# Self-attention of a decoder layer: heads in pairs, scores in two row halves, value product turned round, group norm on transposed outputs

## The chip, the cores and the metric

The kernel runs on one core of a Trainium2 chip. The metric is device time in microseconds (us) of one launch; lower is better. Engines: PE is TensorE (matmuls; its weight loads are shown apart as PEld), DVE is VectorE, ACT is ScalarE, POOL is GpSimd, SP is SyncE, which issues nearly all DMAs here.

## The reference, cut to what matters

One decoder layer on 256 tokens of 1024 features: a SwiGLU half step, self-attention with 16 heads of 64, cross-attention to 256 memory tokens, a second SwiGLU half step, a final norm. The change touches the self-attention alone. For each head h with its queries, keys and values (256 x 64 each) the kernel computes

```
s   = q k^T / 8 + bias(distance) + log(multiplicity)     # -1e30 where the key is later than the query
p   = exp(s - max(s));   o = (p @ v) / sum(p)            # 256 queries x 64
ya  = o of heads 0..11,  times 1/rms over its 768 features, times g_out_a
yb  = o of heads 12..15, times 1/rms over its 256 features, times g_out_b
x   = x + concat(ya, yb) @ w_out
```

The three dilated patterns of heads 0 to 11 fold into one softmax by the log of the number of patterns that reach a key; heads 12 to 15 see one own block of 256 keys. So all 16 heads are the same work with different bias tables.

## The kernel before, in words

Residual x lives transposed (features on partitions, 256 tokens along the row) in eight tiles `X`. Every large product is taken in two float32r parts (a rounded part and the remainder, `split` and `wsplit`), as `mm2` (L201 to L203: one matmul of 512 columns and one of 256) or `mm3` (L185 to L187). Weights come in loads of 0.5 MB; ACT (L122) and DVE (L123) split each into its two parts, up to eight chunks ahead.

The queries and keys of a group of eight heads lie transposed in a slot: head pair j in columns 256 j to 256 j + 255, its even head on partitions 0 to 63 and its odd one on 64 to 127. The values lie with tokens on partitions. These small products are plain float32.

`attend` is side work. The main stream (`qkv(1)` while group 0 attends; `cross_k` and `cross_v(0)` while group 1 does) calls `tick` after each product, which moves a clock in us and fires whatever `later` has put in its list by then. So a head's steps stand between main-stream matmuls in PE's queue. A scheduler then orders the instructions of every engine by its own estimate of when each is ready, and each engine works through its list in that order. For each head:

- `scores` (L448, L449): two matmuls with 64 rows of the array, 128 and 256 columns; DVE adds the bias and takes the maximum (L455, L457); ACT takes exp and the sum (L459).
- `turn` (L466, L469): three 128x128 transposes of p on PE, copied out of PSUM by DVE.
- `pv` (L475 to L477): three matmuls with p^T as the stationary operand (128 columns) and 64 columns of values moving; results gather in two PSUM banks held for the whole group.

After head 7 `finish` divides by the sums. After group 1 `out_norm` takes both groups' sums of squares on ACT, (mean + eps)^-0.5 on POOL, and scales O on DVE; `transposed` then turns O in 16 transposes (L516) and splits it times the gain. `addT(w_out, ..)` follows once all four slots of the result are asked for. `Stats` is the helper for norms on transposed data: `add` squares on ACT and adds on POOL, `_col` sums over partitions by a matmul with ones (L329), takes the power on POOL (L334) and builds two diagonal tiles on DVE (L338); `_rows` spreads them over partitions by a second matmul (L344) that DVE copies out (L346).

Of the kernel before, what the change touches and what calls it, by code (L numbers as in the profile page):

```python
# [13 lines left out]
OP = mybir.AluOpType  # L14
# [14 lines left out]
def layer_kernel(ctx, tc, x_in, mem_in, g_ffn1, w_gu1, w_dn1, g_mix, w_in, rel_bias, g_out_a, g_out_b,  # L29
# [98 lines left out]
    def colchunk(wd, c0, n, nkt=KT):  # L128
        """split tiles of n columns: per k-tile (tile, offset)."""
# [9 lines left out]
    def colchunk2(wd, c0, c1):  # L139
        """256 columns at c0 beside 256 columns at c1."""  # L140
# [49 lines left out]
    def act(slots, k):  # L190
        """hi and lo [128, 256 tokens] of k-tile k."""
# [14 lines left out]
    def mmT(ps, wk, xs, k, blk, start, stop):  # L206
        """ps[128 columns of block blk, 256 tokens] += w^T x for k-tile k, as two halves if ps is [128, 512]."""
# [8 lines left out]
    def mmT_wide(pieces, wk, xs, k, start, stop):  # L216
        """mmT of all blocks, each in its own bank, part by part."""
# [8 lines left out]
    def projT(wk, xs, nblk, spread=False, whole=0, abreast=False):  # L226
        """the transposed product block by block; in halves but for the last blocks."""
# [22 lines left out]
    def halves(out, ps):  # L250
        """out = the sum of the halves of ps."""
# [4 lines left out]
    def scaled(out, pieces, R, scale=None):  # L256
        """out = pieces side by side, times the rows R."""
# [23 lines left out]
    def proj(ps, wk, xs, tb, n=512):  # L281
        """ps[128 tokens of block tb, n columns]."""
# [7 lines left out]
    def split(s, k, nk, src, g=None):  # L290
        """k-tiles k, k + 1, .. of the slot from src [128, nk x 256]."""
# [10 lines left out]
    class Stats:  # L302
        """sum of squares over features, then 1/rms as a column per token block and as rows."""

        def __init__(self):
# [20 lines left out]
        def _col(self):  # L326
# [5 lines left out]
            nc.vector.tensor_scalar(ms, ps[:, 0:4:2], 1.0 / D, 1e-6, OP.mult, OP.add)  # L332
# [26 lines left out]
    def next_x(gname):  # L359
        """splitter of finished residual blocks for the next normalised product."""  # L360
# [53 lines left out]
    def addT(wd, src, block):  # L414
        """X += wd^T src over 8 k-tiles."""
# [22 lines left out]

    def attend(g, q, k, v, O, lsum, every, then=None, wait=1.0):
        """side work: one head after another, `every` us apart."""  # L440
        po = [bank(), bank()]

        def scores(hl):
            h = g * 8 + hl
            rows = slice((hl % 2) * 64, (hl % 2) * 64 + 64)
            o = (hl // 2) * 256
# [4 lines left out]
            pt = work.tile([P, 384], F32, tag="pt", name="pt", bufs=4)  # L451
            mx = small.tile([P, 2], F32, tag="mx", name="mx")
            nm = small.tile([P, 2], F32, tag="nm", name="nm")
            for tb, c, n, fo in ((0, 0, 128, 128), (1, 128, 256, 0)):
                nc.vector.tensor_tensor_reduce(pt[:, c:c + n], sp[:, c:c + n], F[h // 8][:, h % 8, fo:fo + n],  # L455
                                               1.0, -3.0e38, OP.add, OP.max, mx[:, tb:tb + 1])
            nc.vector.tensor_scalar(nm, mx, -1.0, None, OP.mult)  # L457
            for tb, c, n in ((0, 0, 128), (1, 128, 256)):
                nc.scalar.activation(pt[:, c:c + n], pt[:, c:c + n], AF.Exp, bias=nm[:, tb:tb + 1],  # L459
                                     accum_out=lsum[tb][:, h:h + 1])  # L460
            later(4.0, turn, hl, pt)

        def turn(hl, pt):
            tp = bank()
            for i in range(3):
                nc.tensor.transpose(tp[:, i * P:(i + 1) * P], pt[:, i * P:(i + 1) * P], ident)  # L466
            tick(0.33)
            pT = work.tile([P, 384], F32, tag="pT", name="pT", bufs=2)
            nc.vector.tensor_copy(pT, tp[:, :384])  # L469
            later(2.0, pv, hl, pT)  # L470

        def pv(hl, pT):
            oc = slice(hl * 64, hl * 64 + 64)
            oc1 = slice(512 + hl * 64, 512 + hl * 64 + 64)
            nc.tensor.matmul(po[0][:, oc], pT[:, 0:128], v[:, oc], start=True, stop=True)  # L475
# [381 lines left out]
```

## Time and profile before

| what | us |
| --- | --- |
| time, median of 3 runs (lowest to highest) | 627.78 (627.72 to 627.87) |
| profiled execution, its span | 626.8 |
| the median over the span | 0.98 |
| PE busy, share of the span | 616.6, 98% |
| weight loads busy, share | 545.6, 87% |
| DVE, ACT, POOL busy | 443.4, 344.2, 39.1 |
| PE's share of the chain that ended last | 95% |

Busy time of PE is the time in which some matmul was under way; matmuls overlap their fill and drain, so the duration of one is longer than what it adds to the stream. What one adds is read from the starts of its neighbours. The self-attention stands between 235.7 and 336 us of the span.

### The profile page before, as it was taken

How to read it: one execution, taken by the hardware profiler on the slowest of the kernel's cores; microseconds unless marked ns; L12 is line 12 of the kernel's file. 1: busy time of each engine (PE TensorE's matmuls, PEld its weight loads, DVE VectorE, ACT ScalarE, POOL GpSimd, SP SyncE). 2: the span in 40 equal slices, each digit the busy share in tenths (PEclk: the TensorE clock that was granted, in tenths of full speed). 3: DMA queues.
4: the chain of work that ended last, by engine and by line, in shares of the span. 5: the costliest groups of instructions: out<-in, count | busy, mean ns of one | idle time of the engine just before them, and what ended most of it. 6: DMA issues, size and time to landing. Idle time of an engine off the chain costs nothing.

```text
span 626.8 us, 10024 instructions
## 1 busy us (share of the span) xinstructions
PE 616.6 (98%) x3806; PEld 545.6 (87%) x3806; DVE 443.4 (71%) x743; ACT 344.2 (55%) x597; POOL 39.1 (6%) x52
## 2 busy tenths in 40 slices
PE   8999999999999999999999999999999999999996
PEld 7987888888999988887788998889888888889985
DVE  4888648887576665866768797878688787784415
ACT  6766436564555257545566766757464564654313
POOL 0000200000011102100001220003000000000000
PEclk9999999999999999999999999999999999999998
DMA  6867995677565554254335463634555656475401
GB/s 228 282 209 240 218 241 185 210 246 238 185 197 171 166 189 149 79 181 145 101 94 186 158 218 98 192 104 137 196 176 195 201 178 213 147 266 185 155 0 68
DMA packets 58992, 110.07 MB, mean 176 GB/s; under 512 B 3760, under 2 KB 14864, under 8 KB 58944
## 3 DMA queue, kind: packets, MB, share of 16 engines
q1 hardware_dynamic: 57952, 106.02, 52.5%
q0 software_dynamic: 832, 2.88, 2.7%
q8 instruction: 30, 0.49, 0.3%
q10 hardware_dynamic: 160, 0.53, 0.2%
q14 instruction: 18, 0.15, 0.1%
HBM read 107.58 MB, written 1.84 MB: 175 GB/s over the span
## 4 chain that ended last, share of the span: by engine, by line
PE 95%; DVE 1%; issue 1%; DMA 1%; ACT 0%; POOL 0%; POOLq 0%; SPq 0%; DVEq 0%
PE bank L202 38%; PE bank L203 19%; PE bank L185 8%; PE bank L186 8%; PE bank L187 8%; PE bank L222 7%; PE bank L449 1%; PE bank L448 1%; PE bank L466 1%; DMA raw<-in_w_ffn_gu_dram 1%; DVE w L123 1%; PE bank L516 1%; PE bank L477 1%; PE bank L476 1%; PE bank L475 0%
## 5 line engine op out<-in xcount | busy, mean ns | idle before, releaser
L202 PE MATMUL bank<-slot,w 128*128 128x512 f32 x1000 | 358.5, 402 | 0.0
L123 DVE TENSOR_TENSOR w<-raw,w 128x1024 fp32r<-128x1024 f32 (+1 forms) x197 | 237.5, 1218 | 75.6 <-ACT w L122 73.9
L203 PE MATMUL bank<-slot,w 128*128 128x256 f32 x1000 | 281.0, 281 | 0.0
L122 ACT ACTIVATE w<-raw 128x1024 fp32r<-128x1024 f32 (+1 forms) x197 | 202.3, 1050 | 105.0 <-PE bank L187 41.7
L202 PEld LDWEIGHTS bank<-slot,w 128*128 128x128 f32 x1000 | 187.9, 188 | 49.3 <-issue 4.6
L203 PEld LDWEIGHTS bank<-slot,w 128*128 128x128 f32 x1000 | 189.0, 189 | 0.1
L185 PE MATMUL bank<-w,slot 128*128 128x512 f32 (+1 forms) x196 | 67.7, 346 | 0.0
L186 PE MATMUL bank<-w,slot 128*128 128x512 f32 (+1 forms) x196 | 67.2, 343 | 0.0
L187 PE MATMUL bank<-w,slot 128*128 128x512 f32 (+1 forms) x196 | 66.9, 341 | 0.0
L253 ACT ACTIVATE hv<-bank 128x256 f32<-128x256 f32 x108 | 40.2, 375 | 43.0 <-PE bank L203 41.5
L222 PE MATMUL bank<-slot,w 128*128 128x256 f32 x432 | 55.4, 285 | 1.3 <-ACT w L122 1.3
L222 PEld LDWEIGHTS bank<-slot,w 128*128 128x128 f32 x432 | 52.8, 191 | 1.8 <-ACT w L122 1.5
L187 PEld LDWEIGHTS bank<-w,slot 128*128 128x128 f32 x196 | 36.9, 188 | 4.5
L185 PEld LDWEIGHTS bank<-w,slot 128*128 128x128 f32 x196 | 37.0, 189 | 4.4
L186 PEld LDWEIGHTS bank<-w,slot 128*128 128x128 f32 x196 | 37.1, 189 | 3.8
L185 PE MATMUL bank<-slot,w 128*128 128x256 f32 x120 | 34.0, 284 | 0.0
L187 PE MATMUL bank<-slot,w 128*128 128x256 f32 x120 | 34.0, 283 | 0.0
L186 PE MATMUL bank<-slot,w 128*128 128x256 f32 x120 | 34.0, 283 | 0.0
L296 ACT ACTIVATE slot<-u 128x512 fp32r<-128x512 f32 x22 | 13.9, 630 | 34.3 <-DVE u L390 34.2
L254 DVE TENSOR_TENSOR u<-bank,hv 128x256 f32<-128x256 f32 x40 | 16.8, 420 | 13.6 <-ACT hv L253 13.5
L300 DVE SCALAR_TENSOR_TENSOR slot<-X,gT,slot 128x256 fp32r<-128x256 f32 x30 | 21.1, 722 | 5.1 <-ACT slot L299 5.0
L185 PEld LDWEIGHTS bank<-slot,w 128*128 128x128 f32 x120 | 23.0, 192 | 0.1
(140 smaller groups left out, 549.4 us busy)
## 6 DMA issues: line engine op xcount, KB each, us to landing
raw<-in_w_ffn_gu_dram SPq DMA_DIRECT2D x88, 512.0 KB, 4.8
raw<-in_w_ffn_down_dram SPq DMA_DIRECT2D x44, 512.0 KB, 4.4
raw<-in_w_ckv_dram SPq DMA_DIRECT2D x16, 512.0 KB, 4.7
raw<-in_w_in_dram SPq DMA_DIRECT2D x12, 512.0 KB, 3.7
raw<-in_w_in_dram SPq DMA_DIRECT2D x24, 256.0 KB, 4.2
raw<-in_w_out_dram SPq DMA_DIRECT2D x8, 512.0 KB, 4.3
raw<-in_w_cq_dram SPq DMA_DIRECT2D x8, 512.0 KB, 5.5
raw<-in_w_co_dram SPq DMA_DIRECT2D x8, 512.0 KB, 5.2
```

The lines of the kernel that those rows point to most:

```text
L122: nc.scalar.activation(w[:, 0, a:b], raw[:, a:b], AF.Copy)
L123: nc.vector.tensor_tensor(w[:, 1, a:b], raw[:, a:b], w[:, 0, a:b].bitcast(F32), OP.subtract)
L185: nc.tensor.matmul(ps, ah, bh, start=start, stop=False)
L186: nc.tensor.matmul(ps, al, bh, start=False, stop=False)
L187: nc.tensor.matmul(ps, ah, bl, start=False, stop=stop)
L202: nc.tensor.matmul(ps, wh, xhl, start=start, stop=False)
L203: nc.tensor.matmul(ps[:, :256], wl, xhl[:, :256], start=False, stop=stop)
L222: nc.tensor.matmul(ps, w[:, wp_, o + blk * P:o + (blk + 1) * P], a, start=start and i == 0, stop=stop and i == 2)
L253: nc.scalar.activation(t, ps[:, 256:], AF.Copy)
L254: nc.vector.tensor_tensor(out, ps[:, :256], t, OP.add)
L296: nc.scalar.activation(h, src, AF.Copy)
L300: nc.vector.scalar_tensor_tensor(l, src, g, h.bitcast(F32), OP.mult, OP.subtract)
```

## The change

Heads go in pairs. `scores(j)` issues the four matmuls of heads 2j and 2j+1 alternately: 128 columns of the even head (rows 0 to 63 of the array, its own PSUM bank), 128 of the odd (rows 64 to 127, another bank), then 256 and 256. Probabilities are divided by their sum before the transposes, on POOL (32 `tensor_scalar`). `pv(j)` holds 64 columns of values stationary and streams p^T (256 and 128 columns), the even head into partitions 0 to 63 of one bank and the odd into 64 to 127, so that the output is already transposed. No PSUM bank is held over a group. `pv(j)` of pairs 0 and 1 stands right behind the scores of pair j+2; of pairs 2 and 3 some 2.5 us behind their transposes. Of the two copies of p^T one is now ACT's. The norm of the two groups uses `Stats` on the transposed outputs, the first (768 features) after pair 5, the second after pair 7; `out_split` applies 1/rms and gain and splits. `finish`, `out_norm` and the 16 transposes of O go. (The full diff also drops comments and docstrings.)

```
-        def scores(hl):
-            sp = bank()
-            nc.tensor.matmul(sp[:, 0:128], q[rows, o:o + 128], k[rows, o:o + 128], start=True, stop=True)
-            nc.tensor.matmul(sp[:, 128:384], q[rows, o + 128:o + 256], k[rows, o:o + 256], start=True, stop=True)
...
-            later(4.0, turn, hl, pt)
...
-            nc.tensor.matmul(po[0][:, oc], pT[:, 0:128], v[:, oc], start=True, stop=True)
-            nc.tensor.matmul(po[1][:, oc], pT[:, 128:256], v[:, oc], start=True, stop=False)
-            nc.tensor.matmul(po[1][:, oc], pT[:, 256:384], v[:, oc1], start=False, stop=True)
+        def scores(j):
+            rows = (slice(0, 64), slice(64, 128))
+            sp = [bank(), bank()]
+            for c, n, t in ((0, 128, 0), (128, 256, 128)):
+                for e in range(2):
+                    nc.tensor.matmul(sp[e][:, c:c + n], q[rows[e], o + t:o + t + 128], k[rows[e], o:o + n],
+                                     start=True, stop=True)
+            tick(0.6)
+            if j > 1:
+                pv(j - 2)
...
+                nc.vector.reciprocal(rl, l)
+                for tb, c, n in ((0, 0, 128), (1, 128, 256)):
+                    nc.gpsimd.tensor_scalar(pt[:, c:c + n], pt[:, c:c + n], rl[:, tb:tb + 1], 1.0, OP.mult, OP.mult)
+                pts[j].append(pt)
+            later(8.0, turn, j)
...
+        def pv(j):
+            op = bank()[:, :256]
+            for kb, c, n in ((0, 0, 256), (1, 256, 128)):
+                for e in range(2):
+                    vc = kb * 512 + (j * 2 + e) * 64
+                    nc.tensor.matmul(op[e * 64:e * 64 + 64, 256 - n:256], v[:, vc:vc + 64], pTs[j][e][:, c:c + n],
+                                     start=kb == 0, stop=kb == 1)
+            nc.vector.tensor_copy(OT[g][:, j * 256:j * 256 + 256], op)
+            done(g * 4 + j, op)
...
+    def head_pair(kt, op):
+        st = stA if kt < 6 else stB
+        st.add(op)
+        if kt == 5:
+            st.done(delay=3.0)
+            later(8.0, lambda: out_split(OT, stA.rows(), range(3), ot))
+        elif kt == 7:
+            st.done(delay=3.0)
+            later(8.0, lambda: out_split(OT, stB.rows(), range(3, 4), ot))
```

On PE, one head of group 1 as it stood before: scores (L448, L449), a main-stream product (L202, L203: `mm2`), the value product of the head before (L475 to L477).

```order
L448 MATMUL bank<-slot 128x128
L449 MATMUL bank<-slot 128x256
L202 MATMUL bank<-slot,w 128x512
L203 MATMUL bank<-slot,w 128x256
L475 MATMUL bank<-slot,pT 128x64
L476 MATMUL bank<-slot,pT 128x64
L477 MATMUL bank<-slot,pT 128x64
```

On PE now, pair 2 of group 1 at the same place: L451 are the scores of both heads, L498 the value product of pair 0, L202 and L203 the main stream.

```order
L451 MATMUL bank<-slot 128x128 x2
L451 MATMUL bank<-slot 128x256 x2
L498 MATMUL bank<-pT,slot 64x256 x2
L498 MATMUL bank<-pT,slot 64x128 x2
L202 MATMUL bank<-slot,w 128x512
L203 MATMUL bank<-slot,w 128x256
```

Two heads' scores now stand next to each other, alternating between the halves, and the value product of another pair right behind them, with no main-stream product between.

On PE, the end of the attention before: the last products of `cross_v(0)` (L185 to L187: `mm3`) and the 16 transposes of O (L516).

```order
L185 MATMUL bank<-w,slot 128x512
L186 MATMUL bank<-w,slot 128x512
L187 MATMUL bank<-w,slot 128x512
L516 MATMUL bank<-ident,slot 128x128 x16
L185 MATMUL bank<-w,slot 128x512
L186 MATMUL bank<-w,slot 128x512
L187 MATMUL bank<-w,slot 128x512
```

On PE now, the same place: L330 and L345 are the two steps of the second group's `Stats` (L329 and L344 before), and the first L202 is the first product of `addT(w_out, ..)`.

```order
L185 MATMUL bank<-w,slot 128x512
L330 MATMUL bank<-ones,ssq 128x2 x2
L186 MATMUL bank<-w,slot 128x512
L187 MATMUL bank<-w,slot 128x512
L185 MATMUL bank<-w,slot 128x512
L186 MATMUL bank<-w,slot 128x512
L187 MATMUL bank<-w,slot 128x512
L345 MATMUL bank<-dg,ones 128x128 x2
L202 MATMUL bank<-slot,w 128x512
L203 MATMUL bank<-slot,w 128x256
```

The transposes are gone; five matmuls of `cross_v(0)` stand between the two steps of the norm, and behind the second nothing is left of `cross_v(0)`.

On DVE now, what lies around those two steps: L333 turns the sums into mean squares, L339 builds the diagonals, L347 copies the rows R, L513 and L297 are `out_split` of the last two tiles; L123 are weight splits and L584 a split of the cross values.

```order
L333 TENSOR_SCALAR ms<-bank 128x2
L123 TENSOR_TENSOR w<-raw,w 128x1024
L339 TENSOR_SCALAR dg<-ident,col 128x128 x2
L584 SCALAR_TENSOR_TENSOR slot<-bank,col,slot 128x512
L347 COPY R<-bank 128x256
L123 TENSOR_TENSOR w<-raw,w 128x1024
L513 SCALAR_TENSOR_TENSOR og<-slot,gT,R 128x256 x2
L123 TENSOR_TENSOR w<-raw,w 128x1024
L297 TENSOR_TENSOR slot<-og,slot 128x2x256
```

On DVE before, the corresponding place: mean squares (L504) and the scaling of O (L507) of the second block of tokens, then weight splits and the splits of the transposed O (L300).

```order
L504 TENSOR_SCALAR oms<-oss 128x1
L573 SCALAR_TENSOR_TENSOR slot<-bank,col,slot 128x512
L507 TENSOR_SCALAR slot<-slot,or 128x768
L507 TENSOR_SCALAR slot<-slot,or 128x256
L123 TENSOR_TENSOR w<-raw,w 128x1024 x2
L300 SCALAR_TENSOR_TENSOR slot<-bank,gT,slot 128x256 x5
```

A chain through DVE, POOL, DVE, PE, DVE and ACT now ends in `addT`, with three weight splits between its steps.

## Rows read from the trace of the kernel before

**Rows 1.** The page, parts 1 and 2: busy time of each engine; PE's share, granted clock in slices.
```profile
PE 616.6 (98%) x3806; PEld 545.6 (87%) x3806; DVE 443.4 (71%) x743; ACT 344.2 (55%) x597; POOL 39.1 (6%) x52
PE   8999999999999999999999999999999999999996
...
PEclk9999999999999999999999999999999999999998
```

**Rows 2.** The page, part 4: the chain that ended last, by engine.
```profile
PE 95%; DVE 1%; issue 1%; DMA 1%; ACT 0%; POOL 0%; POOLq 0%; SPq 0%; DVEq 0%
```

**Rows 3.** Timeline of PE, one head: start us, us, engine, line, operation, tiles, shape, count.
```profile
303.34 0.28 PE L203 MATMUL bank<-slot,w 128*128 128x256 f32 x1
...
303.70 0.28 PE L203 MATMUL bank<-slot,w 128*128 128x256 f32 x1
303.90 0.49 PE L448 MATMUL bank<-slot 64*128 64x128 f32 x2
304.23 0.59 PE L449 MATMUL bank<-slot 64*128 64x256 f32 x2
304.75 0.50 PE L202 MATMUL bank<-slot,w 128*128 128x512 f32 x1
305.09 0.28 PE L203 MATMUL bank<-slot,w 128*128 128x256 f32 x1
...
306.11 0.28 PE L203 MATMUL bank<-slot,w 128*128 128x256 f32 x1
306.23 0.49 PE L466 MATMUL bank<-ident,pt 128*128 128x128 f32 x3
...
306.79 0.28 PE L203 MATMUL bank<-slot,w 128*128 128x256 f32 x1
```

**Rows 4.** Timeline of the weight loads (PEld) in the same stretch.
```profile
303.90 0.29 PEld L448 LDWEIGHTS bank<-slot 64*128 64x128 f32 x2 [0.25 <-issue]
304.12 0.30 PEld L449 LDWEIGHTS bank<-slot 64*128 64x128 f32 x2
304.75 0.19 PEld L202 LDWEIGHTS bank<-slot,w 128*128 128x128 f32 x1 [0.33 <-issue]
```

**Rows 5.** Timeline of PE, the transposes of O and their neighbours.
```profile
333.94 0.40 PE L187 MATMUL bank<-w,slot 128*128 128x512 f32 x1
334.17 1.91 PE L516 MATMUL bank<-ident,slot 128*128 128x128 f32 x16
...
336.15 0.40 PE L186 MATMUL bank<-w,slot 128*128 128x512 f32 x1
```

**Rows 6.** Timeline of PE, two norms by `Stats` (L329, L344) in the main stream.
```profile
204.86 0.50 PE L329 MATMUL bank<-ones,ssq 128*128 128x2 f32 x4
205.22 3.36 PE L222 MATMUL bank<-slot,w 128*128 128x256 f32 x26
208.42 0.60 PE L344 MATMUL bank<-dg,ones 128*128 128x128 f32 x4
208.78 0.49 PE L222 MATMUL bank<-slot,w 128*128 128x256 f32 x2
...
435.84 0.51 PE L329 MATMUL bank<-ones,ssq 128*128 128x2 f32 x4
...
440.08 0.68 PE L344 MATMUL bank<-dg,ones 128*128 128x128 f32 x4 [0.64 <-DVE dg L338]
```

**Rows 7.** Timeline of DVE between the steps of the first of these norms.
```profile
206.96 0.48 DVE L338 TENSOR_SCALAR dg<-ident,col 128x128 f32<-128x128 f32 x2 [0.83 <-POOL col L334]
```

**Rows 8.** Timeline of ACT, the end of the same head's exp.
```profile
307.08 0.50 ACT L459 ACTIVATE pt<-pt,nm 128x256 f32<-128x256 f32 x1
```

**Rows 9.** Timeline: POOL's addition of squares, and a weight split on DVE beside it.
```profile
251.51 0.73 POOL L317 TENSOR_TENSOR ssq<-ssq,sq 128x256 f32<-128x256 f32 x1 [0.44 <-ACT sq L312]
...
251.65 1.68 DVE L123 TENSOR_TENSOR w<-raw,w 128x1024 fp32r<-128x1024 f32 x1
```

**Rows 10.** Groups by line and shape on DVE, two of them: count, busy us, mean ns.
```profile
L123 DVE TENSOR_TENSOR w<-raw,w 128x1024 fp32r<-128x1024 f32 x195 | 236.1, 1223 | 74.0 <-ACT w L122 72.4 <-DMA rbt<-in_rel_bias_dram 0.5
...
L297 DVE TENSOR_TENSOR slot<-kn,slot 128x512 fp32r<-128x512 f32 x4 | 2.7, 685 | 0.0
```

More of the change, by code (lines that the diff above doesn't have):

```diff
@@ L331, in _col @@
             ms = small.tile([P, 2], F32, tag="ms", name="ms")
-            nc.vector.tensor_scalar(ms, ps[:, 0:4:2], 1.0 / D, 1e-6, OP.mult, OP.add)
+            nc.vector.tensor_scalar(ms, ps[:, 0:4:2], 1.0 / self.n, 1e-6, OP.mult, OP.add)
             self.col = small.tile([P, 2], F32, tag="col", name="col")
@@ L437, in qkv @@
         return q, k, v
-    def attend(g, q, k, v, O, lsum, every, then=None, wait=1.0):
-        po = [bank(), bank()]
-        def scores(hl):
-            h = g * 8 + hl
-            rows = slice((hl % 2) * 64, (hl % 2) * 64 + 64)
-            o = (hl // 2) * 256
-            sp = bank()
-            nc.tensor.matmul(sp[:, 0:128], q[rows, o:o + 128], k[rows, o:o + 128], start=True, stop=True)
-            nc.tensor.matmul(sp[:, 128:384], q[rows, o + 128:o + 256], k[rows, o:o + 256], start=True, stop=True)
-            tick(0.65)
[L451 to L460, printed above, removed]
-            later(4.0, turn, hl, pt)
[L463 to L474, printed above, removed]
-            nc.tensor.matmul(po[0][:, oc], pT[:, 0:128], v[:, oc], start=True, stop=True)
-            nc.tensor.matmul(po[1][:, oc], pT[:, 128:256], v[:, oc], start=True, stop=False)
-            nc.tensor.matmul(po[1][:, oc], pT[:, 256:384], v[:, oc1], start=False, stop=True)
-            tick(0.33)
-            if hl == 7:
-                finish()
-        def finish():
-            for tb in range(2):
-                rl = small.tile([P, 8], F32, tag="rl", name="rl")
-                nc.vector.reciprocal(rl, lsum[tb][:, g * 8:g * 8 + 8])
-                nc.vector.tensor_tensor(O[tb][:, g * 512:g * 512 + 512].rearrange("p (h e) -> p h e", e=64),
-                                        po[tb].rearrange("p (h e) -> p h e", e=64),
-                                        rl.unsqueeze(2).broadcast_to([P, 8, 64]), OP.mult)
-            if then is not None:
-                then()
-        for hl in range(8):
-            later(wait + hl * every, scores, hl)
@@ new lines, in out_split @@
+    def out_split(OT, R, js, ot):
+        for j in js:
+            t = work.tile([P, 512], F32, tag="g1", name="og", bufs=3)
+            for i in range(2):
+                kt = j * 2 + i
+                nc.vector.scalar_tensor_tensor(t[:, i * 256:i * 256 + 256],
+                                               OT[kt // 4][:, (kt % 4) * 256:(kt % 4) * 256 + 256], gain("out", kt),
+                                               R, OP.mult, OP.mult)
+            s = slot()
+            split(s, 0, 2, t)
+            ot.append(s)
@@ L728, in layer_kernel @@
     st.done()
-    O = [slot(F32), slot(F32)]
-    lsum = [work.tile([P, 16], F32, tag=f"l{tb}", name=f"l{tb}", bufs=1) for tb in range(2)]
+    OT = [slot(F32), slot(F32)]
+    stA, stB = Stats(768), Stats(256)
+    ot = []
+    def head_pair(kt, op):
[7 more added lines that the diff above has]
+            later(8.0, lambda: out_split(OT, stB.rows(), range(3, 4), ot))
     qkv0 = qkv(0, xs, st)
-    attend(0, *qkv0, O, lsum, 4.0)
+    attend(0, *qkv0, OT, 7.0, head_pair)
     mxs, mst = mem_side()
     qkv1 = qkv(1, xs, st)
-    ot = []
-    def normed():
-        out_norm(O)
-        later(7.5, transposed, lambda kt, tb: O[tb][:, kt * P:(kt + 1) * P], "out", None, None, ot)
-    attend(1, *qkv1, O, lsum, 3.3, normed)
+    attend(1, *qkv1, OT, 6.0, head_pair)
     K = cross_k(mxs, mst)
```

50 lines of the change are left out of this document (37 added, 13 removed).

## The prediction

> **What bounds the kernel now.** I read the page's busy times first, then the chain that ended last, then PE's timeline. PE is busy 616.6 of 626.8 us with the granted clock at full level in nearly every slice [rows 1], the level of 2.4 GHz, and 95% of the chain that ended last is PE [rows 2]. So the time is the length of PE's list plus what PE waits. DVE has 71%, ACT 55%, POOL 6% [rows 1]: work moved to them costs only if PE comes to wait for it.
>
> What an item adds to PE's list is read from the starts of the main stream's matmuls around it, not from durations. Undisturbed, one L203 follows the last after 0.36 us (303.34 to 303.70) [rows 3]. With a head's scores between them it is 1.39, so scores cost 1.03; with a head's value product 1.02, so 0.66; with three transposes 0.68, so 0.32 [rows 3]. Sixteen heads: 16 x (1.03 + 0.66) = 27.0 us for scores and value products. The transposes of p stay 48 in number and are left out.
>
> **What the 1.03 consists of.** Each plain float32 matmul shows as two records (x2): two passes, each with its own weight load [rows 3, 4]. The two loads of L448 take 0.29 together where one takes 0.19, so loads start 0.1 to 0.11 apart, and a pass of 128 columns also adds 0.11: L448 to L449 is 0.33, one load and two passes. A pass of 256 columns I take as twice that, 0.22; two of them fill 0.44 of the 0.52 from L449 to L202 [rows 3]. The passes of one head make 0.66; the other 0.37 of the 1.03 go in changing to 64 rows and back. The loads sit idle 0.25 before and 0.33 behind the scores for "issue", that is for nothing that waits on another engine [rows 4]; between 128-row matmuls this isn't seen. I call it a change of shape, 0.19 each way.
>
> The Trainium skill (TensorEngine Tiling (Array Packing), Key Properties) says that changing the tiling mode drains the engine. The idle 0.25 and 0.33 agree. By that rule the new value product, with 64 columns stationary, pays as well, though the old one did not; without the rule the sum below would come out up to 3 us lower.
>
> **Scores and value products after.** Two heads have 1.32 of passes for the scores (four of 0.11, four of 0.22), and the value product has the same: two heads of 256 and 128 columns, two passes each. With nothing beside anything a session is 1.32 + 0.37 = 1.69. If the halves were wholly parallel it would be 0.66 + 0.37 = 1.03. Between them: the two passes of one matmul use the same half and follow each other, so only the second pass of one head can lie beside the first pass of the other. In the issued order the value product then takes 0.22 x 3, then 0.11 x 2 = 0.88, with the change 1.25. For the scores the same pairing gives 0.88, but each pass needs a load of 128 columns, and no two loads in rows 4 start closer than 0.1; in line at 0.11 they hold the passes back to 1.09, with the change 1.46. The trace shows neither half next to the other nor a stationary of 64 columns, so both ends stay in the range: 1.03 to 1.69 for each session. For the change of the value product the ends are 0 (the old one) and 0.37; I take 0.37, the row of the other narrow shape. I take the middle case, since the loads' spacing is the nearest row. In four of the eight pairs the value product stands right behind scores, which saves one change out of four each: 4 x 0.19 = 0.7.
>
> Sum: 8 x (1.46 + 1.25) - 0.7 = 21.0, against 27.0: -6.0 us.
>
> **Norm.** The 16 transposes of O cost 2.21 - 2 x 0.23 = 1.75 (L187 at 333.94 to L186 at 336.15, two matmuls apart) [rows 5]. Each new `Stats` adds two items of 0.36 (204.86 to 205.22, 208.42 to 208.78) [rows 6], two of them 1.4. Net -0.3.
>
> **New waits of PE.** None of the old steps made PE wait noticeably. Now:
> - Second group's norm. Between L330 and L345 stand five matmuls, so L345 is due 0.36 + 5 x 0.23 = 1.5 behind L330. In the trace the diagonals were done 2.6 behind L329 at best (207.44 to 204.86) [rows 6, 7], and at worst L344 came 4.24 behind, after a wait of 0.64 shown on the weight loads [rows 6]. A weight split (1.22) [rows 10] stands between the same steps on DVE's list now. PE waits 1.1 to 2.7; I take 2.0, and everything behind it in PE's list, `addT`, waits along.
> - The last tile of `out_split`. It is asked for 12 products, 4.3 us, behind L345. The chain is L345 0.4, the copy of R 0.4, a weight split 1.2, two scalings 0.8, a second weight split 1.2 beside ACT's rounding, and the subtraction 0.7 [rows 10] (the pieces of 256 columns are taken as 0.4, from the 0.69 of 512): 4.7. 0 to 1.2; I take 0.5.
> - First group's norm. Its last addition on POOL stands behind the scaling of pair 7's probabilities. 0 to 1.0; 0.5.
> - Transposes of a pair. One head's exp ended 3.7 us behind the start of its scores (307.58 to 303.90) [rows 3, 8]. For the second head of a pair add its longer scores 0.7, its place behind the first on DVE 0.9, a weight split in front of its reciprocal 1.2, and on POOL 0.4 + 0.7 for each head (the 0.73 of an addition over 256 columns as upper bound [rows 9], less below): 8.7. In the order some 19 main products and two sessions lie between, 9.5 us. So it is hidden with 0.8 to spare, less than one weight split of 1.22. Over eight pairs 0 to 6; I take 1.0.
>
> Together +4.0. ACT and DVE gain some 2 us of work each over the 100 us of the attention, POOL about 24; DVE at 71% and POOL nearly idle there cover this, and without that cover it would come as the last wait in the list.
>
> Sum: -6.0 - 0.3 + 4.0 = -2.3. The profiled execution has a span of 626.8 and the median is 627.8, 1.0 around it; the same around the new span gives 627.8 - 2.3 = **625.5**.
>
> **Rivals.**
> 1. The halves are wholly parallel, or nearly. Scores and value products take 8 x 2.06 - 0.7 = 15.8: -11.2, with the rest 620.3. For it: two heads touch disjoint rows and banks. Against: in rows 3 and 4 a half-height matmul still shows both passes and both loads in line. The Trainium skill (TensorE: Matmul & The Clock Gate, Part 3: Packing small matmuls) states for tiles in different row groups that they start about 4 ns apart and take little more than one of them; by it alone the two heads' scores would cost one head's. No run here shows that yet. Chance 0.17.
> 2. Slower: nothing overlaps. Sessions of 1.69 make 8 x 3.38 - 0.7 = 26.3, -0.7 in all, and the waits of +4.0 decide: 627.8 - 0.7 - 0.3 + 4.0 = 630.8. It decides as soon as the overlap gives under 3.3 of its 6 us. For it: a load and a pass of the same head stand between any two instructions of different heads but one, and in rows 3 and 4 everything of L448 and L449 goes in line. Chance 0.17.
> 3. Only the row halves overlap, the value product doesn't, since both its heads need all 128 rows: 8 x (1.46 + 1.69) - 0.7 = 24.5, -2.5; 629.0. Chance 0.12.
> 4. The softmax comes late. A weight split took 1.68 instead of 1.22 beside an addition of POOL [rows 9, 10]: the two engines hold each other up. With 32 scalings more on POOL and the margin of 0.8 above, each pair would be 1 us late: 8 instead of 1: 632.5. The Trainium skill (SBUF — State Buffer, Who interferes with whom) says that a DVE instruction with two inputs in SBUF and a GpSimd one that reads SBUF exclude each other; the 1.68 agrees. Chance 0.10.
>
> **How the numbers follow.** The forecast has 0.44, over 623 to 628 with its waits of 1 to 6. What a measurement of this kernel can tell from no change is 0.2%, 1.3 us, so faster means below 626.5 and slower above 629.0. Faster: 0.33 of the forecast, 0.17 of rival 1, 0.01 of rival 3: 0.51. Within 0.2%: 0.09 of the forecast, 0.02 of rival 2, 0.06 of rival 3, 0.01 of rival 4: 0.18. Slower: 0.02 of the forecast, 0.15 of rival 2, 0.05 of rival 3, 0.09 of rival 4: 0.31. The range reaches from rival 1 to rival 2: 620.5 to 630.8.
>
> **What will show it.** L451: sessions of about 1.5 us for two heads, from L203 to L203 less 0.36, with the odd head's first pass starting at the even head's second. L498: 1.25, with idle loads for "issue" around it. L345: a wait of about 2 us for the diagonals on DVE. L482: waits for POOL in few pairs. The prediction is wrong if sessions stand near 1.03 or 1.69, if PE waits more than 6 us between 235 and 340, or if that stretch of PE's list changes elsewhere.

## The result, and the profile after

| what | us |
| --- | --- |
| time after, median of 4 runs (lowest to highest) | 623.1 (621.92 to 624.2) |
| before, beside it | 627.82 (627.72 to 627.87) |
| ratio | 0.9923, 95% interval 0.9912 to 0.9935 |
| profiled execution of after, its span | 623.77, 622.0 |

Faster by 4.7 us, where 2.3 were forecast. Page of after, parts 1 and 2, against [rows 1]:

```profile
PE 608.2 (98%) x3774; PEld 536.5 (86%) x3774; DVE 443.2 (71%) x755; ACT 345.7 (56%) x601; POOL 61.7 (10%) x90
...
PE   8999999999999999899998999999999999999995
...
PEclk9999999999999999999997999999999999999999
```

PE is busy 8.4 us less, but the span is only 4.8 shorter: there are two slices with an 8 in PE's row where there was none, and the clock row has a 7. Part 4, against [rows 2], shows PE's share of the chain fallen from 95% to 91%:

```profile
PE 91%; DVE 2%; ACT 2%; issue 2%; POOL 1%; DMA 1%; POOLq 0%; SPq 0%; DVEq 0%; ACTq 0%
```

**Scores and value products.** Timeline of PE, the value product of a pair alone, the scores of a pair alone, and further on the scores of a pair with the value product of another behind them (compare [rows 3]):

```profile
276.17 0.39 PE L187 MATMUL bank<-w,slot 128*128 128x512 f32 x1
276.49 0.87 PE L498 MATMUL bank<-pT,slot 128*64 128x256 f32 x8
277.29 0.50 PE L185 MATMUL bank<-w,slot 128*128 128x512 f32 x1
277.63 0.40 PE L186 MATMUL bank<-w,slot 128*128 128x512 f32 x1
...
284.19 0.28 PE L203 MATMUL bank<-slot,w 128*128 128x256 f32 x1
284.40 0.93 PE L451 MATMUL bank<-slot 64*128 64x128 f32 x8
285.26 0.50 PE L202 MATMUL bank<-slot,w 128*128 128x512 f32 x1
285.59 0.28 PE L203 MATMUL bank<-slot,w 128*128 128x256 f32 x1
...
297.55 0.28 PE L203 MATMUL bank<-slot,w 128*128 128x256 f32 x1
297.76 0.93 PE L451 MATMUL bank<-slot 64*128 64x128 f32 x8
298.61 0.87 PE L498 MATMUL bank<-pT,slot 128*64 128x256 f32 x8
299.41 0.50 PE L202 MATMUL bank<-slot,w 128*128 128x512 f32 x1
299.75 0.28 PE L203 MATMUL bank<-slot,w 128*128 128x256 f32 x1
```

From L203 to L203 the scores of two heads take 1.40, less 0.36: 1.04 (1.05 in the mean of four). One head took 1.03 before. The eight records of two heads are busy for 0.93; the four of one head, L448 and L449 of [rows 3], reach from 303.90 to 304.82, 0.92. So the second head costs next to nothing (0.01 to 0.02). In the single records behind the row both heads' first passes start 0.007 apart, then both second passes, and so on; the loads likewise. The value product of a pair alone adds 0.99 to 1.00 (here 1.46 from L187 to L186, less two steps of 0.23); scores and value product together add 1.85 (2.20 less the 0.35 of an undisturbed step), 0.19 less than apart.

Timeline of the weight loads in the second of these stretches, against [rows 4]:

```profile
297.75 0.52 PEld L451 LDWEIGHTS bank<-slot 64*128 64x128 f32 x8 [0.26 <-issue]
298.61 0.63 PEld L498 LDWEIGHTS bank<-pT,slot 128*64 128x64 f32 x8 [0.33 <-DVE w L123]
```

The idle time at each change of shape is still there, 0.26 and 0.33 as before. (That 0.33 is named after a DVE split, but the same 0.33 stands as "issue" behind scores without a value product.)

Over the eight pairs scores and value products take 15.6 us, where the sixteen heads took 27.2: -11.6.

**Where part of it went.** PE at the norm of the second group, after (L330 and L345 are L329 and L344 of [rows 6]):

```profile
326.42 0.39 PE L185 MATMUL bank<-w,slot 128*128 128x512 f32 x1
327.45 0.61 PE L330 MATMUL bank<-ones,ssq 128*128 128x2 f32 x4 [0.64 <-POOL ssq L318]
...
328.92 0.40 PE L187 MATMUL bank<-w,slot 128*128 128x512 f32 x1
331.27 1.23 PE L345 MATMUL bank<-dg,ones 128*128 128x128 f32 x4 [1.95 <-DVE dg L339]
...
333.57 0.63 PE L202 MATMUL bank<-slot,w 128*128 128x512 f32 x1
334.00 0.41 PE L203 MATMUL bank<-slot,w 128*128 128x256 f32 x1
334.21 0.63 PE L202 MATMUL bank<-slot,w 128*128 128x512 f32 x1
```

POOL and DVE between the two steps:

```profile
329.28 1.61 POOL L335 TENSOR_TENSOR col<-ms,mhalf 128x2 f32<-128x2 f32 x1 [1.89 <-DVE ms L333]
```
```profile
329.06 0.14 DVE L333 TENSOR_SCALAR ms<-bank 128x2 f32<-128x2 f32 x1
329.13 1.21 DVE L123 TENSOR_TENSOR w<-raw,w 128x1024 fp32r<-128x1024 f32 x1
330.93 0.48 DVE L339 TENSOR_SCALAR dg<-ident,col 128x128 f32<-128x128 f32 x2 [0.59 <-POOL col L335]
```

L330 to L345 is 3.8 us: DVE reaches the mean 1.6 after L330, POOL's power takes 1.6 beside a weight split, and the diagonals follow. Five products (1.2 us) cover it. L330 costs 0.9 more than the 0.44 that such a step adds without a wait (0.36 for itself, 0.08 on the product behind it), the wait at L345 2.2. And then the products are slow: L202 to L202 is 0.64 (333.57 to 334.21) instead of 0.35. Stretches of 2 us there, with the granted clock in the third column from the right:

```profile
330.00:332.00 2.00, 0.73 (x3) 0.73 (x4) 1.41 (x4) 0.04 (x1) 0.90 (x1) 0.57 0.75 250
332.00:334.00 2.00, 2.00 (x8) 1.71 (x7) 1.54 (x3) 1.06 (x1) 0.00 (x0) 0.50 0.73 215
...
336.00:338.00 2.00, 2.00 (x11) 1.75 (x10) 1.75 (x3) 0.00 (x0) 0.00 (x0) 0.72 0.69 221
```

While PE waits for the diagonals the clock falls to 0.50, the level of 1.2 GHz, and stays there until 337: 0.7 at L345 itself and 0.27 on each of seven products, 2.6 us. In the profiled execution of before, the clock was down only at the start and the end.

At the memory norm, which existed before, L345 now waits too. PE, then POOL:

```profile
258.78 0.28 PE L203 MATMUL bank<-slot,w 128*128 128x256 f32 x1
260.52 0.68 PE L345 MATMUL bank<-dg,ones 128*128 128x128 f32 x4 [1.46 <-DVE dg L339]
```
```profile
258.71 0.70 POOL L335 TENSOR_TENSOR col<-ms,mhalf 128x2 f32<-128x2 f32 x1 [4.96 <-DVE ms L333]
```

That is 1.7 us beyond the step's own 0.44, and the clock stays up here. The second pair's transposes lose 0.9 more: in the trace they wait for L254 on DVE, that for L253 on ACT, and that for POOL's additions of squares, three in 4.10 us at 249.66. A value product before them loses 0.3.

**The account.** From the 401st to the 561st L202, in which all of this lies, before took 125.9 us and after 123.3: -2.6. The parts give -11.6 + 0.9 + 2.2 + 2.6 + 1.7 + 0.9 + 0.3 = -3.0; the remaining 0.4 I can't place. The other 2.1 of the 4.8 lie where the change touched nothing: 0.8 at two small products of the bias table near 56 us, for which PE waited in the profiled execution of before, and 1.3 in the last gate and up product, which ran at another pace. Groups of PE there, 500 to 530 of before and 495 to 525 of after, where neither waits (busy us, mean ns):

```profile
L202 PE MATMUL bank<-slot,w 128*128 128x512 f32 x86 | 30.4, 399 | 0.0
```
```profile
L202 PE MATMUL bank<-slot,w 128*128 128x512 f32 x88 | 30.6, 391 | 0.0
```

The same instructions at the same granted clock of full speed: 0.3533 us from one L202 to the next in the one, 0.3467 in the other, 1.9%. More on this at the end.

### The profile page after: what moved, and what is told of

It is laid out like the page before. It is cut to its first block, busy times and chain, and to the rows that moved or that the text cites. A ratio compares the mean times of both kernels' runs of the same rounds, so it can differ in the third digit from the quotient of the medians.

```text
span 622.0 us, 10043 instructions
## 1 busy us (share of the span) xinstructions
PE 608.2 (98%) x3774; PEld 536.5 (86%) x3774; DVE 443.2 (71%) x755; ACT 345.7 (56%) x601; POOL 61.7 (10%) x90
## 4 chain that ended last, share of the span: by engine, by line
PE 91%; DVE 2%; ACT 2%; issue 2%; POOL 1%; DMA 1%; POOLq 0%; SPq 0%; DVEq 0%; ACTq 0%
PE bank L202 38%; PE bank L203 19%; PE bank L185 8%; PE bank L186 8%; PE bank L187 8%; PE bank L222 7%; PE bank L451 1%; PE bank L498 1%; DVE w L123 1%; DMA raw<-in_w_ffn_gu_dram 1%; PE bank L345 1%; ACT w L122 1%; PE bank L482 1%; POOL ssq L318 1%; POOL col L335 1%
## 5 line engine op out<-in xcount | busy, mean ns | idle before, releaser
L202 PE MATMUL bank<-slot,w 128*128 128x512 f32 x1000 | 357.3, 401 | 0.0
L123 DVE TENSOR_TENSOR w<-raw,w 128x1024 fp32r<-128x1024 f32 (+1 forms) x197 | 237.6, 1220 | 78.3 <-ACT w L122 77.1
L203 PE MATMUL bank<-slot,w 128*128 128x256 f32 x1000 | 281.3, 281 | 0.0
L122 ACT ACTIVATE w<-raw 128x1024 fp32r<-128x1024 f32 (+1 forms) x197 | 202.1, 1050 | 105.7 <-PE bank L187 44.4
L202 PEld LDWEIGHTS bank<-slot,w 128*128 128x128 f32 x1000 | 188.8, 189 | 46.9 <-issue 2.5
L203 PEld LDWEIGHTS bank<-slot,w 128*128 128x128 f32 x1000 | 190.1, 190 | 0.2
L185 PE MATMUL bank<-w,slot 128*128 128x512 f32 (+1 forms) x196 | 67.7, 346 | 0.0
L186 PE MATMUL bank<-w,slot 128*128 128x512 f32 (+1 forms) x196 | 67.3, 343 | 0.0
L187 PE MATMUL bank<-w,slot 128*128 128x512 f32 (+1 forms) x196 | 66.9, 341 | 0.0
L253 ACT ACTIVATE hv<-bank 128x256 f32<-128x256 f32 x108 | 39.9, 375 | 37.5 <-PE bank L203 34.1
L222 PEld LDWEIGHTS bank<-slot,w 128*128 128x128 f32 x432 | 52.8, 191 | 1.2 <-ACT w L122 0.9
L185 PEld LDWEIGHTS bank<-w,slot 128*128 128x128 f32 x196 | 36.9, 188 | 4.8 <-issue 0.3
L187 PEld LDWEIGHTS bank<-w,slot 128*128 128x128 f32 x196 | 36.9, 188 | 4.5
L186 PEld LDWEIGHTS bank<-w,slot 128*128 128x128 f32 x196 | 37.1, 189 | 3.9
L185 PE MATMUL bank<-slot,w 128*128 128x256 f32 x120 | 34.0, 284 | 0.0
L187 PE MATMUL bank<-slot,w 128*128 128x256 f32 x120 | 34.0, 283 | 0.0
L186 PE MATMUL bank<-slot,w 128*128 128x256 f32 x120 | 34.0, 283 | 0.0
L296 ACT ACTIVATE slot<-u 128x512 fp32r<-128x512 f32 x22 | 13.9, 630 | 33.5 <-DVE u L391 33.4
L318 POOL TENSOR_TENSOR ssq<-ssq,sq 128x256 f32<-128x256 f32 x28 | 24.0, 859 | 61.9 <-ACT sq L313 61.3
L254 DVE TENSOR_TENSOR u<-bank,hv 128x256 f32<-128x256 f32 x40 | 16.8, 420 | 13.9 <-ACT hv L253 13.8
L300 DVE SCALAR_TENSOR_TENSOR slot<-X,gT,slot 128x256 fp32r<-128x256 f32 x30 | 21.1, 721 | 4.5 <-ACT slot L299 4.4
```

What stands on the lines that cost most here:

```text
L122: nc.scalar.activation(w[:, 0, a:b], raw[:, a:b], AF.Copy)
L123: nc.vector.tensor_tensor(w[:, 1, a:b], raw[:, a:b], w[:, 0, a:b].bitcast(F32), OP.subtract)
L185: nc.tensor.matmul(ps, ah, bh, start=start, stop=False)
L186: nc.tensor.matmul(ps, al, bh, start=False, stop=False)
L187: nc.tensor.matmul(ps, ah, bl, start=False, stop=stop)
L202: nc.tensor.matmul(ps, wh, xhl, start=start, stop=False)
```

## Experiments

The runs stand in three lots, each beside the kernel before: `e1` to `e4` (627.39 us), `r1` to `e8` (627.64), `e10` and `e11` (627.74). Besides the time I give the stretch from the 401st to the 561st L202 of each profiled execution, which leaves the pace of the other stages out: 125.9 before. It belongs to one execution, the median to all of them.

| run | median us | ratio (95%) | stretch us |
| --- | --- | --- | --- |
| after | 623.1 | 0.9923 (0.9912 to 0.9935) | 123.3 |
| `e1_head_after_head` | 623.77 | 0.9936 (0.9917 to 0.9955) | 123.6 |
| `e2_scores_only` | 622.71 | 0.9925 (0.9912 to 0.9939) | 120.7 |
| `e3_value_and_norm_only` | 624.15 | 0.9948 (0.9935 to 0.9962) | 122.9 |
| `e4_late_norm` | 625.16 | 0.9962 (0.9949 to 0.9975) | 117.5 |
| `r1_after_again` | 623.09 | 0.9933 (0.9916 to 0.9949) | 122.1 |
| `e5_scale_on_vectore` | 624.70 | 0.9945 (0.9931 to 0.9958) | 124.2 |
| `e7_earlier_last_pair` | 620.80 | 0.9885 (0.9872 to 0.9898) | 120.2 |
| `e8_filled_wait` | 620.93 | 0.9893 (0.9881 to 0.9906) | 120.7 |
| `e11_late_memory_norm` | 620.86 | 0.9879 (0.9859 to 0.9899) | 119.0 |
| `e10_all_waits_covered` | 617.15 | 0.9832 (0.9818 to 0.9845) | 116.5 |

**1. Do the halves run side by side because neighbours in the list alternate?** `e1_head_after_head` issues all matmuls of the even head ahead of the odd head's, in both products:

```
-            for c, n, t in ((0, 128, 0), (128, 256, 128)):
-                for e in range(2):
+            for e in range(2):
+                for c, n, t in ((0, 128, 0), (128, 256, 128)):
```

> The changed kernel, but in each pair all matmuls of the even head stand in PE's list before those of the odd head, for the scores and for the value product. Theory A, neighbours: a pass runs beside a pass of the other half only where the two stand next to each other in the list, so only one pass of eight overlaps: a session of scores goes from 1.05 to 1.5-1.6 us, one of the value product from 1.00 to 1.45-1.6, in all +7 to +9: 630-632. Theory B, a list for each half: passes of the two heads find each other wherever they stand: sessions stay 1.05 and 1.00, time 622-624.

Measured: scores of a pair 1.05 to 1.06, value product 1.00, the two together 1.86 to 1.87 instead of 1.85: theory B. The row of a pair's scores reads as in after:

```profile
284.57 0.93 PE L451 MATMUL bank<-slot 64*128 64x128 f32 x8
```

In the single records the odd head's passes start 0.013 to 0.014 behind the even head's, not behind its last one, which starts 0.54 later. That this is twice the 0.007 of after fits one more matmul of the even head listed in front; the list itself stands in no view. The two halves run as if each had its own list, and the order of the two heads hardly counts.

**2. The two halves of the change alone.** `e2_scores_only` is the kernel before with `scores` for two heads at once, four matmuls in alternation as in after; value product, norm on O and the rest are the old ones:

```
-        for hl in range(8):
-            later(wait + hl * every, scores, hl)
+        for j in range(4):
+            later(wait + 2 * j * every, scores, j)
```

> The kernel before with the scores alone in pairs; value product head by head with p^T stationary, division by the sum and norm on O as before. Theory A, sessions plus waits: eight sessions of 1.05 in place of sixteen of 1.04, -8.2, and without POOL's scalings and the two norms none of the new waits: 627.8 - 8.2 = 619.6 (619-621), below the changed kernel. Rival, the waits come from two heads' softmax at once on DVE and ACT: PE waits in the transposes, 3 or more us of the 8.2 lost: 622.5 or more.

Measured 622.71: the whole gain of the change, with half of it. The sessions give 8.2 (8 x 1.05 for 16 x 1.03 to 1.04), the stretch 5.2. Most of the rest turns up behind attention, at the old norm (1.0 and 0.8):

```profile
330.87 0.50 PE L202 MATMUL bank<-slot,w 128*128 128x512 f32 x1 [0.76 <-DVE slot L300]
...
333.18 0.50 PE L202 MATMUL bank<-slot,w 128*128 128x512 f32 x1 [0.63 <-DVE slot L300]
```

The time of the rival came, but not its place: the splits of the transposed result are late, not the transposes of p. In the kernel before the same steps made PE wait for nothing. PE's list ahead of them has become shorter, the chain through DVE and ACT has not.

`e3_value_and_norm_only` is after with scores head by head, a planner microsecond apart:

```
-                for e in range(2):
-                    nc.tensor.matmul(sp[e][:, c:c + n], q[rows[e], o + t:o + t + 128], k[rows[e], o:o + n],
-                                     start=True, stop=True)
+                nc.tensor.matmul(sp[e][:, c:c + n], q[rows[e], o + t:o + t + 128], k[rows[e], o:o + n],
+                                 start=True, stop=True)
```

> The changed kernel with the scores of each head by themselves again (two sessions 1 us apart), all else as changed. Theory A, sessions plus waits: scores +8.2 against the changed kernel, the value product keeps 8 x 1.00 + shared changes, the waits of the norms and POOL stay (+6): 630.5-632, slower than before. Rival, the waits come from paired scores: they go, and it ends at 625-627.

Measured 624.15, below both ranges. The value product of a pair takes 0.99 in it as well, so the column halves run side by side without paired scores; L330 still waits 0.55, L345 of the second group not at all, and the clock stays up:

```profile
333.03 0.61 PE L345 MATMUL bank<-dg,ones 128*128 128x128 f32 x4
```

My theory, that the waits belong to the new norm, fell: the same norm waits 2.5 us less when PE's list is 8 us longer. Fourteen matmuls of `cross_v(0)`, not five, stand between its two steps there.

**3. Where are the waits to be taken out?** `e4_late_norm` puts the second group's norm later and lets `addT` run over the six finished k-tiles of all four blocks first:

```
-            st.done(delay=3.0)
-            later(8.0, lambda: out_split(OT, stB.rows(), range(3, 4), ot))
+            st.done(delay=6.0, gap=4.0)
+            later(10.5, lambda: out_split(OT, stB.rows(), range(3, 4), ot))
...
-    until(lambda: len(ot) == 4)
+    until(lambda: len(ot) >= 3)
```

> The changed kernel with the second group's norm later and further apart in PE's list (first step 6 us behind the last value product, the second 4 us behind that), and addT going over k-tiles 0 to 5 of all four blocks first, so that the last tile of out_split is asked for 24 products behind the start. Theory A: the waits of 0.9 at L330 and 2.9 at L345 in the profile of the changed kernel go: -3 to -3.8, 619.3-620.1. Rival, the chain through DVE and POOL is late for addT wherever it stands: the wait moves to the first product of k-tile 6, gain under 1 us, 622-623.

Measured 625.16, 2 us worse than after. L330 and L345 stand at 0.44, as hoped, but the last tile is later still. PE and ACT:

```profile
341.29 0.50 PE L202 MATMUL bank<-slot,w 128*128 128x512 f32 x1 [2.56 <-DVE slot L297]
```
```profile
338.32 1.06 ACT L122 ACTIVATE w<-raw 128x1024 fp32r<-128x1024 f32 x1 [2.39 <-DMA raw<-in_w_cq_dram]
339.28 0.61 ACT L296 ACTIVATE slot<-og 128x512 fp32r<-128x512 f32 x1
```

ACT's list goes in order, and a weight split of the next stage that waits for its DMA stands ahead of the rounding that PE needs. Then the four blocks end together and the next norm waits 2.4 us for the last sum of squares, and behind that wait the clock is down as well (0.50 from 364 to 366), some 1.5 us by the starts of the products there. From the 561st L202 to the end it is 286.1, where after has 279.1. The rival's number was 622 to 623; both were too low.

**4. Is it the POOL engine?** `e5_scale_on_vectore` scales p on DVE:

```
-                    nc.gpsimd.tensor_scalar(pt[:, c:c + n], pt[:, c:c + n], rl[:, tb:tb + 1], 1.0, OP.mult, OP.mult)
+                    nc.vector.tensor_scalar(pt[:, c:c + n], pt[:, c:c + n], rl[:, tb:tb + 1], None, OP.mult)
```

> The changed kernel with the scaling of p by its row sum on VectorE instead of GpSimd; nothing else. Theory A (GpSimd's list, longer by 32 scalings, holds up the memory norm's pow and the sums of squares): the 1.7 us before the memory norm's dg product and the 0.9 us before the second pair's transposes go, and the time falls by about 2.5 us against the changed kernel, to 620 to 621.5 us. Rival B (VectorE, busy for 443 of 622 us, has no room for 32 scalings more just where the splits of the weights and the softmax meet): the waits come back at the transposes and splits, and the time is within 1 us of the changed kernel or above it.

Measured 624.70, 1.6 above after in the same lot: rival B. The waits at the memory norm and at the second pair's transposes do not shrink; PE at the memory norm, of this kernel:

```profile
260.67 0.46 PE L345 MATMUL bank<-dg,ones 128*128 128x128 f32 x2 [1.86 <-DVE dg L339]
```

So the scalings on POOL were not the cause of these waits; in after POOL had been idle for 4.96 before its power there. DVE does the scaling in 0.28 and 0.35 each, and the diagonals now stand behind that on DVE's list. Behind this wait the clock falls too (0.54 from 262 to 264), which it does not do there in after, so part of the 1.6 may be the clock.

**5. What does the fallen clock cost by itself?** The changed kernel once more, without an edit:

> The changed kernel once more, word for word, as the measure for the three runs beside it. Both theories: 622 to 624 us, with the granted clock at 0.5 again for some 7 us from the start of the second group's dg product on.

Measured 623.09. L345 waits 2.2 as in after, but the clock was down for less than 4 us behind it, not 7, and the stretch is 1.2 shorter:

```profile
330.00:332.00 2.00, 0.80 (x6) 0.75 (x7) 1.41 (x5) 0.00 (x0) 0.82 (x1) 1.00 0.70 244
332.00:334.00 2.00, 2.00 (x8) 1.71 (x7) 2.00 (x5) 1.06 (x1) 0.00 (x0) 0.52 0.70 221
334.00:336.00 2.00, 2.00 (x10) 1.73 (x9) 2.00 (x4) 0.63 (x1) 0.00 (x0) 0.62 0.57 186
```

`e8_filled_wait` puts nine products, whose result isn't used, where PE waits:

```
         def _rows(self):
+            if self.n == 256:
+                fill = bank()
+                for _ in range(9):
+                    nc.tensor.matmul(fill[:, :P], ident, ident, start=True, stop=True)
```

> The changed kernel with nine products of the identity with itself (their result isn't used) just ahead of the second group's dg product, so that TensorE works through most of its 1.95 us of waiting there. Theory A (the fallen clock is a cost of its own, set off by that wait): the dg product starts at the same time as before, the granted clock stays at full speed behind it, and the time falls by about 2.6 us, to 620 to 621.5 us. Rival B (what follows was waiting for VectorE and ScalarE anyway, so that slower products cost nothing): within 0.5 us of the changed kernel, with new waits of 2 us or more at the last tile of the output projection.

PE of this kernel (L349 is L345), then one of its windows:

```profile
326.96 0.61 PE L330 MATMUL bank<-ones,ssq 128*128 128x2 f32 x4 [0.64 <-POOL ssq L318]
...
327.98 2.17 PE L346 MATMUL bank<-ident 128*128 128x128 f32 x18
...
330.79 0.71 PE L349 MATMUL bank<-dg,ones 128*128 128x128 f32 x4
```
```profile
330.00:332.00 2.00, 2.00 (x13) 1.49 (x12) 1.55 (x4) 0.75 (x2) 0.41 (x1) 1.00 0.63 218
```

L330 to L349 is 3.83, as L330 to L345 was (3.82): the chain has not moved. The clock stays at full speed, and the time falls by 2.2 us against the changed kernel in the same lot, 1.4 in the stretch. Theory A. Over whole executions the mean granted clock was 0.997 to 0.999 in the four of this kernel, 0.991 to 0.996 in all ten of the changed one. Work that does nothing made the kernel faster.

**6. Work that does something in the same place.** `e7_earlier_last_pair`:

```
-            st.done(delay=3.0)
-            later(8.0, lambda: out_split(OT, stB.rows(), range(3, 4), ot))
+            st.done(delay=5.0, gap=3.6)
+            later(10.0, lambda: out_split(OT, stB.rows(), range(3, 4), ot))
...
-    attend(1, *qkv1, OT, 6.0, head_pair)
+    attend(1, *qkv1, OT, 5.0, head_pair)
```

> The changed kernel with the pairs of the second group begun 5.0 instead of 6.0 planner microseconds apart, and the second group's norm told to come 5.0 and 8.6 instead of 3.0 and 5.8 after its last value product: behind that product there stand 24 and 18 products of the cross-attention's value projection ahead of the norm's two steps, where the changed kernel has 25 and 5, and so some 3 us more of cover for the dg product. Theory A (what the change gives back is the bare wait at this norm, together with the clock that falls behind it): the 2.9 us at the dg product go to under 0.5, the clock stays at full speed, and the time falls by 4.5 to 5.5 us, to 617.5 to 619 us. Rival B (the lists of VectorE and ScalarE behind attention are the bound; the wait only moves to the last tile of the output projection, as it did when the norm was put later): 621.5 to 624 us.

Measured 620.80, half of theory A's gain. L345 takes its own 0.44 and the clock stays up, but the first group's L345 now loses 0.9, a pair's value product 0.4, and the last tile 1.2, where ACT's rounding again stands behind a weight split that waited 2.15 for its DMA:

```profile
334.45 0.50 PE L202 MATMUL bank<-slot,w 128*128 128x512 f32 x1 [1.05 <-DVE slot L297]
```

`e11_late_memory_norm` changes one number of after, the place of the memory norm's second step:

```
-                st.done(delay=8.0)
+                st.done(delay=8.0, gap=6.0)
```

> The changed kernel with the memory norm's dg product alone put later (6.0 instead of 2.8 behind its column step; behind a pair's scores and value product and seven products more). Theory A: its 1.7 us of waiting go and nothing takes their place, 621 to 622 us against 623.1 for the changed kernel. Rival B: the pair's scores and value product, which now come 3 us earlier, wait for the softmax of the pair before in its place, and the time is within 0.5 us of the changed kernel.

Measured 620.86: theory A, a little below its range. The memory norm's wait is gone, and the second group's norm is as late as ever, yet the clock did not fall in the profiled execution. PE and its window:

```profile
262.12 0.60 PE L345 MATMUL bank<-dg,ones 128*128 128x128 f32 x4
...
329.17 0.71 PE L345 MATMUL bank<-dg,ones 128*128 128x128 f32 x4 [1.95 <-DVE dg L339]
```
```profile
330.00:332.00 2.00, 2.00 (x13) 1.78 (x12) 2.00 (x4) 1.06 (x1) 0.00 (x0) 1.00 0.72 238
```

So the wait of 1.95 is not enough by itself to bring the clock down; what else decides is open. It differs between executions of this one kernel: the mean granted clock was 0.998 in the two fastest of five (618.21 and 619.07, the profiled one) and 0.993 to 0.995 in the others (620.86 to 621.73), as low as in the changed kernel. The stretch of 119.0 belongs to a fast one.

`e10_all_waits_covered` is the version that the experiments point to: `e7_earlier_last_pair` with three more numbers of the planner:

```
-                st.done(delay=8.0)
+                st.done(delay=8.0, gap=6.0)
...
-            st.done(delay=3.0)
+            st.done(delay=3.0, gap=3.8)
...
-            later(10.0, lambda: out_split(OT, stB.rows(), range(3, 4), ot))
+            later(9.2, lambda: out_split(OT, stB.rows(), range(3, 4), ot))
```

> The changed kernel with the earlier pairs of the last run (5.0 apart; the second group's norm at 5.0 and 8.6) and three small moves in the planner's times: the memory norm's dg product 6.0 instead of 2.8 behind its column step, so that a pair's scores and value product and seven products more stand ahead of it; the first group's dg product 3.8 instead of 2.8 behind; and the last tile of the output projection at 9.2, so that ScalarE rounds it before a weight split that waits for its DMA. Theory A (each wait is a step that PE reaches too early, and work put ahead of it takes its place): the 1.7 us at the memory norm, 0.9 at the first group's norm and 1.05 at the last tile go, 3 to 3.6 us less than the kernel with the earlier pairs alone (620.8; 619.07 in its profiled run), 616 to 618 us. Rival B (the lists of ScalarE, VectorE and GpSimd are full there, and a wait put off comes back at the pair's own transposes or splits): 619.5 to 622 us.

Measured 617.15 (615.55 to 617.58), 6 us under the changed kernel and 10.6 under the kernel before: theory A. PE at the second step of the second group's norm, without a wait for the diagonals:

```profile
325.65 0.61 PE L345 MATMUL bank<-dg,ones 128*128 128x128 f32 x4
```

The waits at the memory norm, the first group's norm and the last tile are gone as well; for the last tile ACT rounds (L296, 328.48) ahead of the weight split that waits for its DMA (L122, 330.01). Its stretch is 116.5, 9.4 under before: of the -11.6 that the sessions give, most is kept. (The profiled execution, 615.55, is the fastest of the five.) No arithmetic was changed against after, only when each step is asked for.

## Why the prediction came out as it did

The forecast of 625.5 was 2.4 us above the time, inside its range, and the sign was right; but two of its terms were wrong by more than the sum, and in opposite directions: the overlap by 5.6, the waits by 4.6. That the sum came out near is luck, and by the prediction's own sign of being wrong (sessions near 1.03) its mechanism for the overlap failed.

- **The overlap: the step that failed.** "The two passes of one matmul use the same half and follow each other, so only the second pass of one head can lie beside the first pass of the other", and loads "in line at 0.11". Sessions of 1.46 and 1.25 came from it; 1.05 and 0.99 were measured, and -11.6 instead of -6.0. The passes of one head do follow each other. But the step made the other half wait for them, as if one list served both, and the records show the second head's passes 0.007 behind the first's, or 0.013 with the heads one after the other in the list (experiment 1). The spacing of the loads, read from one half [rows 4], does not hold between halves. This was rival 1, held at 0.17, and its price of 1.03 for each session was exact to 0.04. The Trainium skill (TensorE: Matmul & The Clock Gate, Part 3: Packing small matmuls) gives about 4 ns from tile to tile; here it is 7 ns. The same part says that matmuls start in strict order of the program; in experiment 1 the odd head's first pass started 0.31 ahead of the even head's second matmul, which the edit lists in front of it.
- **The change of shape** held: 0.39 beside 0.66 of passes for the scores, 0.33 for the value product (0.37 in the forecast), and 0.19 saved where the two stand together (1.85 against 1.04 + 0.99).
- **The norm**: -0.3 expected, none measured. The two added steps take 0.44 each time, not 0.36, which left out the 0.08 on the product behind.
- **The waits: mis-sized, 8.6 instead of 4.0** (6.0 of bare waits and 2.6 of clock). The chain at L345 was named with its place and its engines, 2.0 against 2.2. What the term left out: 0.9 at L330 before it, 1.7 at the memory norm, which the change leaves as it was, and above all 2.6 of a clock that falls behind the wait. The waits foreseen for `out_split` and for the first group's norm, 0.5 each, did not come; those of the transposes and products of a pair, 1.0, were 1.2.
- **Rival 2 and rival 3** (no overlap, row halves alone) are refuted by the 1.05 and the 0.99. **Rival 4**, the softmax late through POOL and DVE, too: weight splits took 1.22 us in the mean before and after, and the waits did not go when POOL was relieved (experiment 4). The hold-up itself shows at POOL's power: 1.61 at the second group's norm, where it starts 0.15 behind a weight split, 0.70 at the memory norm, where it starts 0.12 ahead of one.
- **The sum** for the attention: -2.3 forecast, -2.6 measured in the stretch (-3.8 in `r1_after_again`, whose clock was down for a shorter time). In the two profiled executions 2.1 us of the 4.8 come from stages that are the same in both kernels.

The wider error lies in the direction of thought: I priced waits by the new steps, one by one. Experiments 2 and 3 show that they come, at least in part, from what was removed. Behind the 8 us taken from PE's list stand chains on DVE, ACT and POOL that have kept their length, and a step of them that PE meets sooner than before can be a new wait, in old code too (1.0 and 0.8 in experiment 2).

## What to carry to other kernels

When matmuls fill half of the array, put two of them in the two halves, rows or columns: the second was nearly free here, in either order, as long as the pair stands together, so that the change of shape is paid once. When work is cut from the list of the bounding engine, look for the steps that wait for other engines and move them later, behind work that is ready; here that was worth more than the change itself (6 us against 4.7) and cost six numbers. And an order of side work on an in-order engine is as important as its amount: one weight split that waits for its DMA, ahead of a rounding, cost experiment 3 a wait of 2.6 us.

## What the runs showed of the hardware

- Both heads' float32 passes and weight loads run side by side in row halves (1.05 us for two heads, 1.04 for one) and column halves (0.99 for two); the second head's passes start 0.007 behind the first's.
- The granted clock fell to 0.50 at or just behind a wait of 2.2 us in the middle of a kernel whose PE is busy 98%, and stayed there for 3 to 7 us, at 0.64 instead of 0.35 us for a pair of products. In the profiled execution of `e11_late_memory_norm` the same wait left it at 1.00.
- A stream of matmuls without any wait runs at one of two paces under the same granted clock, 0.3533 or 0.3467 us for an L202 with its L203, and can keep its pace for a whole stage (some 200 pairs, 1.2 to 1.3 us). The kernel before and `e2_scores_only` had the slow one in the last gate and up product, and so had `e1_head_after_head`; the other kernels the fast one. In `e4_late_norm`, `e7_earlier_last_pair` and `e10_all_waits_covered` it also held from some 93 us to 166 us, ahead of anything that they changed, worth 1.2 us. In these three it sets in behind a weight load that waited 0.2 to 0.3 us for a weight split (in `e7_earlier_last_pair` at 92.64); no load of before or after waits so in that stage. So in these the pace changed behind a short pause; what chooses it otherwise is open. Differences of one microsecond between two kernels are therefore to be read from a stretch, not from the total.
